# Projection, scalar and gate products of two token groups: plain fp32 in place of three split products

## The chip, the cores and the metric

The kernel runs on one core of one Trainium2 chip. The metric is the device time of one execution in microseconds (us), the median of several runs. The engines are named as in the profile: PE is TensorE (PEld its weight loads), DVE is VectorE, ACT is ScalarE, POOL is GpSimd, SP is SyncE, which here issues most DMAs. A measurement of this kernel can tell about 0.3% (13 us) from no change.

## The reference

One transformer layer on 1024 tokens plus 16 meta tokens, width 1024, in float32: a mixer with two branches of 8 heads (a gated delta rule, "gdn", and a forgetting attention, "fox"), then a feed-forward layer that looks up 16 experts for each of 8 heads and token ("peer"). Cut to what matters here:

```python
proj = h @ w_in                       # h = rms_norm(res); projections, 24 scalars, gates
qkv_a, z_a, b_a, a_a, qkv_b, f_b, gates = split_cols(proj, IN_SIZES)
...
o_a = rms_norm(gated_delta_rule(...), o_norm_a) * silu(z_a)
o_b = forgetting_attention(...)
y = einsum('blgc,gcd->blgd', o, w_branch)
res = res + sum(sigmoid(gates) * y, axis=2) @ w_out
# peer_ffn: route by top_k, then for the 128 (head, k) pairs of a token
act = gelu(einsum('thkd,td->thk', expert_u[idx], xb))
out = einsum('thk,thkd->td', gate_w * act, expert_v[idx])
```

## The kernel before

The eight blocks of 128 tokens are worked in three groups, blocks 0 to 1, 2 to 4 and 5 to 7 (`GROUPS`, line 26). In the code they are g = 0, 1, 2, in this text groups 1, 2 and 3. `mixer(g)` takes a group through these stages: the projections and the 8 heads (`scalars`, `proj_a`, `conv`, `proj_b`, `gdn`, `fox`, `gates`), the branches, the merge by `w_out`, and the ranking by `w_q`. While the merge and the ranking run, `prologue` normalises and transposes the next group's input into hT. For blocks 0 to 4 the experts are then gathered row by row: POOL issues a gather of 128 rows of `expert_u` or `expert_v`, DVE multiplies and sums the first kind (tiles G, h2p), and PE sums the second kind (`pv<-G,Zb`). This work is spread over all stages from the end of group 1 on. Blocks 5 to 7 go over all experts densely at the end (`dense`: `ua` over `u_t`, then `acc` over `expert_v`).

Products of width are made from two planes. A float32 value is split into a high part hi (rounded to fp32r, an fp32 form that PE takes in one pass) and a low part lo, and a product is hi·hi + hi·lo + lo·hi (`mm`, lines 411 to 420). The inputs' planes are in hT, which holds two planes of [128, 8, 384]. The weights are split as they come: `weights` (line 366) loads a piece wraw on SP's queue, ACT casts it to whi, and DVE or POOL, whichever the planner holds to be free sooner, subtracts to get wlo (line 393). A piece is one of eight k-slices of `w_a` (three 128-column parts of a head), `w_b` (four parts) or a gate slab `w_g`. The ring holds 7 raw pieces and 3 split ones, two pieces are split ahead of use (`D1`, line 62).

No order is written out by hand. `Weave` (line 223) is a planner that runs while the program is recorded: each stage is a generator, and the next step is that with the earliest ready time by the planner's own clocks and durations (`Engine`, `pe_time` and the like). Ties go by `prio`: gdn, then fox, then the projections, then the gates. So the projections fill what PE time the heads leave. Each engine then executes its instructions strictly in the recorded order and waits where an operand is not there.

Of the kernel before, what the change touches and what calls it, by code (L numbers as in the profile page):

```python
# [7 lines left out]
F32 = mybir.dt.float32  # L8
F32R = mybir.dt.float32r
# [4 lines left out]
OP = mybir.AluOpType  # L14
# [258 lines left out]
def _build(ctx, tc, nc, a, groups, dbg, peer):  # L273
# [86 lines left out]
    def bank(tag):  # L360
        return pl.ps.tile([P, 512], F32, name=tag, bufs=pl.banks[tag])
# [3 lines left out]

    def weights(srcs, by=None):


        size, RAW, RING, AHEAD = pl.depth
        todo = [(src, k, size // src.shape[-1]) for src in srcs for k in range(0, 8, size // src.shape[-1])]  # L370
        raws, have = [], []

        def room(t, i):
            src, k, n = todo[i]
            c = src.shape[-1]
            return t[:, :n * c].rearrange("p (k c) -> p k c", c=c)

        def load(n):
            while len(raws) < min(n, len(todo)):
                src, k, m = todo[len(raws)]  # L380
                raw = room(pl.wp.tile([P, size], F32, name="wraw", bufs=RAW), len(raws))
                sp.dma_start(raw, src[:, k:k + m, :])
                raws.append(raw)

        def fetch(n):
            while len(have) < min(n, len(todo)):
                i = len(have)
                load(i + RAW)
                raw = raws[i]
                hi = room(pl.wp.tile([P, size], F32R, name="whi", bufs=RING), i)  # L390
                lo = room(pl.wp.tile([P, size], F32R, name="wlo", bufs=RING), i)
                act.copy(hi, raw)
                (by or (pool if clk.t["pool"] + size * PCOST < clk.t["dve"] + size * 0.001 + PSL else dve)).tensor_tensor(lo, raw, hi, op=OP.subtract)
                raws[i] = None
                have.append((hi, lo))
        used = [0]

        def take():
            first = used[0]
            m = todo[first][2]  # L400
            used[0] += 8 // m

            def w(x, k, c0=0, c1=None):
                return have[first + k // m][x][:, k % m, c0:c1]
            w.need = lambda k: fetch(first + k // m + AHEAD)
            w.flat = lambda x: have[first][x].rearrange("p k c -> p (k c)")
            return w
        take.start = lambda: fetch(AHEAD)
        return take

    def mm(w, *sets):

        for k in range(8):
            w.need(k)
            for ps, lhs, rhs, then in sets:
                for n, (x, y) in enumerate(((0, 0), (0, 1), (1, 0))):
                    pe.matmul(ps, lhsT=lhs(x, k), rhs=rhs(y, k), start=(k == 0 and n == 0), stop=(k == 7 and n == 2))
                yield clk.when("pe", [w(x, k + 1) for x in range(2)], []) if k < 7 and lhs is sets[-1][1] else clk.t["pe"]
        for s in sets:
            s[3]()  # L420
# [43 lines left out]

    def rows_T(x, p, T8, c0, tag):

        for i in range(2):
            v = blocks(bank(tag))
            for k in range(4):
                tr(v[:, k, :p], x[:, (4 * i + k) * P:(4 * i + k + 1) * P], p)  # L470
            put(T8, slice(4 * i, 4 * i + 4), slice(c0, c0 + p), v[:, :, :p])
            yield
# [10 lines left out]
    def group(g):  # L483
        b0, b1 = groups[g]
        q = SimpleNamespace(g=g, b0=b0, nb=b1 - b0, mo=NM if g == 0 else 0, nkp=0 if g == 0 else NM + b0 * P)
        q.nw = q.nb * P
        q.T = q.mo + q.nw
        q.nbm = q.nb + (1 if q.mo else 0)
        q.last = b1 == NBLK
        q.two = 2 if g == 0 else 1  # L490
        q.bs = [(j, P, q.mo + j * P, b0 + j) for j in range(q.nb)]
        q.slots = ([(q.nb, NM, 0, -1)] if q.mo else []) + q.bs
        q.fl = PB[2] if g else 2
        return q

    def mixer(g):
        q = group(g)
        fl, b0, b1 = q.fl, q.b0, q.b0 + q.nb
        with ExitStack() as st:
# [7 lines left out]
                                + [a["w_o"][:, :, i * 512:(i + 1) * 512] for i in range(2)]  # L507
                                + [a["w_q"][:, :, i * 256:(i + 1) * 256] for i in range(8)])
            pl.banks = {"prj": PB[0], "bf": PB[1]} if g else {"prj": 3, "bf": 3}
# [3 lines left out]
            with sb("p0") as hp:  # L513
                q.oT = [hp.tile([P, 8, q.nw], F32, name=f"oT{br}") for br in range(0 if g else 2)]
                q.tok = lambda j: (lambda x, k: hT[:, x, k, q.mo + j * P:q.mo + (j + 1) * P])
                q.sg1 = hp.tile([P, 8, q.nw], F32, name="sg1") if g == 0 else None
                with sb("p1") as q.wk, banks("ps1") as pl.ps:
# [5 lines left out]
                    with sb("p1h") as q.wk:  # L523
# [17 lines left out]
                        for i in range(GF if g else 6):  # L541
                            wv.add(n("gates", i), gates(q, i // 3, i % 3), [n("gates", i - 1) if i else n("pb", H - 1)],
                                   prio=4)
                        wv.run(names + [n("gates", i) for i in range(GF if g else 6)])
                if g:
                    yp = st.enter_context(tpool(f"y_{g}", side="right", reuse_waits="tile"))
                    q.yF = yp.tile([P, 8, q.nw], F32, name="yF")
# [42 lines left out]
    def prologue(q, px, tags):  # L590
# [5 lines left out]
        for ss_ in batches:  # L596
# [10 lines left out]
            if q.mo:  # L607
                raw = px.tile([P, 8, 32], F32, name="wsr")
                act.dma_start(raw, a["w_s"])
            yield clk.when("act", xs[:1], [])  # L610
# [10 lines left out]
            if q.mo:  # L621
                act.copy(ws[0], raw)
                dve.tensor_tensor(ws[1], raw, ws[0], op=OP.subtract)
            yield
            for i, (j, C, c0, b) in enumerate(ss_):
                yield from rows_T(xs[i][:C], C, hT, c0, tags[at % len(tags)])
                at += 1

    def scalars(q):

        wk, g, n3 = q.wk, q.g, q.nbm
        if q.mo:
            act.activation(negA, negA, AF.Exp)
            dve.tensor_scalar(negA, negA, -1.0, None, op0=OP.mult)
            dve.tensor_scalar(qn, qn, P ** -0.5, None, op0=OP.mult)
        ps = bank("prj")
        for k in range(8):
            for n, (x, y) in enumerate(((0, 0), (0, 1), (1, 0))):
                pe.matmul(ps[:32, :q.T], lhsT=ws[x][:, k, :], rhs=hT[:, y, k, :q.T], start=(k == 0 and n == 0),
                          stop=(k == 7 and n == 2))  # L640
            yield clk.t["pe"]
# [72 lines left out]
    def proj_a(q, c, h):  # L714

        wk, T = q.wk, q.T
        wa = q.weights()
        raw = [wk.tile([P, T + 3], F32, name=f"raw{ty}", bufs=RW) for ty in range(3)]

        c.raw = raw  # L720

        def take(ps, ty):
            act.copy(raw[ty][:, 0:3], hal[:, ty, h, :])
            act.copy(raw[ty][:, 3:3 + T], ps[:, :T])
            act.copy(hal[:, ty, h, :], raw[ty][:, T:T + 3])
# [23 lines left out]
    def proj_b(q, c, h):  # L749
# [24 lines left out]
        for (j, C, c0, b) in q.slots:  # L774
            ps = bank("prj")
            if b < 0:
                sets.append((ps[:, 0:256], lambda x, k: hT[:, x, k, 0:P], lambda y, k: wb(y, k, 128, 384),
                             lambda ps=ps, j=j: meta(ps, j)))
            else:
                sets.append((ps, q.tok(j), lambda y, k: wb(y, k), lambda ps=ps, j=j, b=b: real(ps, j, b)))  # L780
# [279 lines left out]
    def gates(q, br, c):  # L1060
# [3 lines left out]
        def then(ps, i):  # L1064
# [80 lines left out]
    def rank(q):  # L1145
# [247 lines left out]
    def dense(b0, nb, held):  # L1393
# [5 lines left out]
        wscr = [dram.tile([P, P, P], F32, name=f"wscr{j}") for j in range(nb - 1)]  # L1399
        wt = ctx.enter_context(tpool("wt", side="right", reuse_waits="tile"))  # L1400
        W = []
        kept = wt.tile([P, NH, nw], F32, name="kept")
        with tpool("p4", reuse_waits="tile") as wk, \
# [4 lines left out]
            def inner():  # L1408
                for c in range(P):
# [8 lines left out]
                    ps = bank("ua")[:, :nw]  # L1418
                    yield from mm(w, (ps, lambda x, k: w(x, k), lambda y, k: hT[:, y, k, :nw], lambda: then(ps)))

# [176 lines left out]
```

## Time and profile before

| | us |
|---|---|
| time before, median of 3 runs | 4275.21 (4273.79 to 4283.71) |
| the profiled execution | 4281.61 |
| its span | 4279.9 |
| PE busy | 3785.7 (88%) |
| DVE busy | 2993.9 (70%) |
| POOL busy | 2265.0 (53%) |
| ACT busy | 1848.3 (43%) |

The share of busy time is a mean over stages that differ. Two stretches matter here. **Stretch A** is the projections, heads and gates of group 2, from its first scalar product (648.7 us) to the first branch product (1421.5 us). **Stretch B** is the same of group 3 (1719.9 to 2587.8 us). Together they are 1640.7 us, 38% of the span. A PE matmul's end is modelled in the profile, and matmuls overlap in the pipeline, so PE's busy time holds the tail of each; the time from one start to the next in a dense run is what a product occupies. A plain fp32 product stands in the trace as two matmul records, an fp32r one as one.

### The profile page before, as it was taken

To read this page: it belongs to the slowest core of one execution; us is meant where nothing else is said; L and a number is where in the kernel's file an instruction comes from. 1 tells how busy PE (TensorE), PEld (TensorE's weight loads), DVE (VectorE), ACT (ScalarE), POOL (GpSimd) and SP (SyncE) were. 2 spreads that over 40 slices of the span, in tenths; PEclk is the share of its full clock that TensorE was granted. 3 is DMA by queue.
4 is the path that set the end of the run, shared out by engine and by line. 5 is a ranking of instruction groups with operands and counts; after the bars stand their busy time and mean duration, and the time that the engine had idled before them with its cause. 6 is when DMAs were issued, how large, how long until landed. Compare 5 with 4: busy or idle time off the path is not lost. (4 is left out here: it accounts for less than half of the span.)

```text
span 4279.9 us, 65388 instructions
## 1 busy us (share of the span) xinstructions
PE 3785.7 (88%) x21126; PEld 2963.2 (69%) x21126; DVE 2993.9 (70%) x8230; ACT 1848.3 (43%) x4588; POOL 2265.0 (53%) x1935
## 2 busy tenths in 40 slices
PE   6999977888888978788898889779999998999998
PEld 5777866666656756556665567568888887776665
DVE  5565479989885667788788656579769565874443
ACT  4665443445443332344444433227666573332222
POOL 3222544665665656566575566564324354764553
PEclk9999988989999989899999999899999999999999
DMA  3232466677788988788788799888989999999997
GB/s 105 87 99 84 137 209 201 223 250 233 239 292 300 334 312 273 259 292 284 268 287 303 258 314 325 313 282 299 321 287 327 332 338 310 390 380 345 340 346 275
DMA packets 525066, 1161.20 MB, mean 271 GB/s; under 512 B 55281, under 2 KB 261137, under 8 KB 524337
## 3 DMA queue, kind: packets, MB, share of 16 engines
q0 software_dynamic: 186960, 679.04, 45.6%
q1 hardware_dynamic: 302464, 457.86, 31.8%
q10 hardware_dynamic: 35296, 20.12, 1.6%
q8 instruction: 166, 2.72, 0.3%
q14 instruction: 180, 1.47, 0.1%
HBM read 1081.73 MB, written 75.07 MB: 270 GB/s over the span
## 5 line engine op out<-in xcount | busy, mean ns | idle before, releaser
L185 POOL DMA_INDIRECT G<-in_expert_v_dram,idxT x640 | 729.9, 1141 | 729.0 <-PE pv L185 376.0
L185 POOL TENSOR_TENSOR wlo<-wraw,whi 128x384 fp32r<-128x384 f32 (+2 forms) x518 | 697.0, 1350 | 775.9 <-ACT whi L185 668.2
L185 POOL DMA_INDIRECT G<-in_expert_u_dram,idx x640 | 744.8, 1164 | 438.4 <-DVE G L185 144.1
L185 ACT CAST whi<-wraw 128x512 fp32r<-128x512 f32 (+2 forms) x1152 | 709.9, 629 | 596.6 <-PE prj L185 203.8
L185 DVE TENSOR_TENSOR wlo<-wraw,whi 128x512 fp32r<-128x512 f32 (+2 forms) x634 | 512.5, 815 | 609.1 <-ACT whi L185 522.1
L185 DVE SCALAR_TENSOR_TENSOR G<-G,h2p 128x1024 f32<-128x1024 f32 x618 | 800.6, 1299 | 64.6 <-DMA G<-in_expert_u_dram,idx 53.2
L185 PE MATMUL prj<-hT,whi 128*128 128x384 f32 (+2 forms) x2176 | 582.9, 354 | 43.6 <-ACT whi L185 33.2
L185 PE MATMUL ua<-hT,whi 128*128 128x384 f32 x2048 | 537.2, 343 | 16.9 <-ACT whi L185 16.9
L185 PE MATMUL pv<-G,Zb 128*32 128x512 f32 x2560 | 409.6, 622 | 54.2 <-DMA G<-in_expert_v_dram,idxT 52.6
L185 PEld LDWEIGHTS prj<-hT,whi 128*128 128x128 f32 x2176 | 384.4, 200 | 86.6 <-ACT whi L185 43.1
L185 PE MATMUL prj<-whi,hT 128*128 128x512 f32 (+1 forms) x1152 | 435.5, 417 | 3.8 <-ACT whi L185 2.7
L185 PEld LDWEIGHTS ua<-hT,whi 128*128 128x128 f32 x2048 | 364.8, 190 | 57.1 <-issue 35.2
L185 PE MATMUL prj<-hT,wlo 128*128 128x384 f32 (+2 forms) x1088 | 369.7, 340 | 24.4 <-POOL wlo L185 16.9
L185 PE MATMUL ua<-hT,wlo 128*128 128x384 f32 x1024 | 346.3, 338 | 4.0 <-DVE wlo L185 3.2
L185 PE MATMUL acc<-whi,Chi 128*128 128x512 f32 x768 | 311.2, 405 | 9.1 <-ACT whi L185 9.1
L185 PE MATMUL acc<-wlo,Chi 128*128 128x512 f32 x768 | 300.8, 392 | 1.8 <-POOL wlo L185 1.6
L185 PE MATMUL acc<-whi,Clo 128*128 128x512 f32 x768 | 300.4, 391 | 0.0
L185 PEld LDWEIGHTS prj<-whi,hT 128*128 128x128 f32 x1152 | 220.4, 194 | 52.9 <-issue 7.4
L185 PE MATMUL prj<-wlo,hT 128*128 128x512 f32 (+1 forms) x576 | 227.1, 394 | 24.2 <-POOL wlo L185 21.4
L185 PEld LDWEIGHTS prj<-hT,wlo 128*128 128x128 f32 x1088 | 215.2, 198 | 41.5 <-POOL wlo L185 31.0
L185 PEld LDWEIGHTS acc<-whi,Chi 128*128 128x128 f32 x768 | 144.7, 188 | 114.6 <-issue 75.5
L185 PEld LDWEIGHTS ua<-hT,wlo 128*128 128x128 f32 x1024 | 193.7, 189 | 8.2 <-DVE wlo L185 8.0
(316 smaller groups left out, 6912.9 us busy)
## 6 DMA issues: line engine op xcount, KB each, us to landing
wraw<-in_u_t_dram SPq DMA_DIRECT2D x256, 256.0 KB
wraw<-in_expert_v_dram SPq DMA_DIRECT2D x128, 512.0 KB
wraw<-in_w_b_dram SPq DMA_DIRECT2D x192, 256.0 KB
wraw<-in_w_a_dram SPq DMA_DIRECT2D x192, 192.0 KB
wraw<-in_w_q_dram SPq DMA_DIRECT2D x96, 256.0 KB
gscr<-Gl SPq DMA_DIRECT2D x122, 192.0 KB
Gr<-gscr SPq DMA_DIRECT2D x122, 192.0 KB
wraw<-in_w_g_dram SPq DMA_DIRECT2D x96, 192.0 KB
```

The lines of the kernel that those rows point to most:

```text
L185: return f(*a, **k)
```

## The change

In groups 2 and 3 the products with `w_a`, `w_b`, `w_g` and the 24 scalar columns are made of the whole float32 values: one plain fp32 product in place of three fp32r ones, and no whi and wlo for these weights. `weights` gets a count `whole`, the number of leading sources that are handed on as the raw piece. The inputs of groups 2 and 3 lie whole in a new buffer hW, half the size of hT; the planes of group 1 go to hT0, which lives only through group 1, and those for the ranking of group 3 and the dense phase to hD. Group 1, the branches, the merge, the ranking and the dense phase still use split products.

```diff
         size, RAW, RING, AHEAD = pl.depth
-        todo = [(src, k, size // src.shape[-1]) for src in srcs for k in range(0, 8, size // src.shape[-1])]
+        todo = [(src, k, size // src.shape[-1], i < whole) for i, src in enumerate(srcs)
+                for k in range(0, 8, size // src.shape[-1])]
...
                 i = len(have)
                 load(i + RAW)
                 raw = raws[i]
+                if todo[i][3]:
+                    have.append((raw,))
+                    continue
                 hi = room(pl.wp.tile([P, size], F32R, name="whi", bufs=RING), i)
                 lo = room(pl.wp.tile([P, size], F32R, name="wlo", bufs=RING), i)
                 act.copy(hi, raw)
@@ -397,11 +401,12 @@
...
         for k in range(8):
             w.need(k)
             for ps, lhs, rhs, then in sets:
-                for n, (x, y) in enumerate(((0, 0), (0, 1), (1, 0))):
-                    pe.matmul(ps, lhsT=lhs(x, k), rhs=rhs(y, k), start=(k == 0 and n == 0), stop=(k == 7 and n == 2))
-                yield clk.when("pe", [w(x, k + 1) for x in range(2)], []) if k < 7 and lhs is sets[-1][1] else clk.t["pe"]
+                pairs = ((0, 0),) if w.whole else ((0, 0), (0, 1), (1, 0))
+                for n, (x, y) in enumerate(pairs):
+                    pe.matmul(ps, lhsT=lhs(x, k), rhs=rhs(y, k), start=(k == 0 and n == 0),
+                              stop=(k == 7 and n == len(pairs) - 1))
+                yield clk.when("pe", [w(x, k + 1) for x in range(1 if w.whole else 2)], []) if k < 7 and lhs is sets[-1][1] else clk.t["pe"]
...
+            if plain:
+                copy(T8[:, 4 * i:4 * i + 4, c0:c0 + p], v[:, :, :p])
+            else:
+                put(T8, slice(4 * i, 4 * i + 4), slice(c0, c0 + p), v[:, :, :p])
...
+        q.hx = (lambda x, k, c0, c1: hW[:, k, c0:c1]) if g else (lambda x, k, c0, c1: hT0[0][:, x, k, c0:c1])
...
+                                whole=2 * H + len(gb[0]) if g else 0)
...
-                q.tok = lambda j: (lambda x, k: hT[:, x, k, q.mo + j * P:q.mo + (j + 1) * P])
+                if not g:
+                    hT0.append(planes(hp, "hT0", q.T))
+                    ws.extend(hp.tile([P, 8, 32], F32R, name=f"ws{i}") for i in range(2))
+                q.tok = lambda j: (lambda x, k: q.hx(x, k, q.mo + j * P, q.mo + (j + 1) * P))
...
+                if q.last and last < NBLK:
+                    hD.append(planes(held.enter_context(tpool("hD", side="right", reuse_waits="tile")), "hD", q.nw))
...
-                yield from rows_T(xs[i][:C], C, hT, c0, tags[at % len(tags)])
+                yield from rows_T(xs[i][:C], C, hW if q.g else hT0[0], c0, tags[at % len(tags)], q.g > 0)
...
+        pairs = ((0, 0),) if g else ((0, 0), (0, 1), (1, 0))
         for k in range(8):
-            for n, (x, y) in enumerate(((0, 0), (0, 1), (1, 0))):
-                pe.matmul(ps[:32, :q.T], lhsT=ws[x][:, k, :], rhs=hT[:, y, k, :q.T], start=(k == 0 and n == 0),
-                          stop=(k == 7 and n == 2))
+            for n, (x, y) in enumerate(pairs):
+                pe.matmul(ps[:32, :q.T], lhsT=wsF[:, k, :] if g else ws[x][:, k, :], rhs=q.hx(y, k, 0, q.T),
+                          start=(k == 0 and n == 0), stop=(k == 7 and n == len(pairs) - 1))
...
-            sets.append((ps[:, :T], lambda x, k, ty=ty: wa(x, k, ty * P, ty * P + P), lambda y, k: hT[:, y, k, :q.T],
+            sets.append((ps[:, :T], lambda x, k, ty=ty: wa(x, k, ty * P, ty * P + P), lambda y, k: q.hx(y, k, 0, q.T),
...
-        yield from wide(q, c1 - c0, lambda y, k: hT[:, y, k, q.mo:q.T], then)
+        yield from wide(q, c1 - c0, lambda y, k: q.hx(y, k, q.mo, q.T), then)
...
-        h2T = hT if b0 >= last else planes(wk, "h2T", q.nw)
+        h2T = hD[0] if b0 >= last else planes(wk, "h2T", q.nw)
...
-        wt = ctx.enter_context(tpool("wt", side="right", reuse_waits="tile"))
+        wt = ctx.enter_context(tpool("wt", reuse_waits="tile"))
...
-    hp = held.enter_context(tpool("hT", reuse_waits="tile"))
-    hT = planes(hp, "hT", max(group(g).T for g in range(len(groups))))
-    ws = [hp.tile([P, 8, 32], F32R, name=f"ws{i}") for i in range(2)]
+    inp = ExitStack()
+    hp = inp.enter_context(tpool("hT", reuse_waits="tile"))
+    hW = hp.tile([P, 8, max(group(g).nw for g in range(len(groups)))], F32, name="hW")
+    wsF = hp.tile([P, 8, 32], F32, name="wsF")
+    hT0, ws, hD = [], [], []
     for g in range(len(groups)):
         mixer(g)
+    inp.close()
```

The order of instructions follows from the planner. On PE, at the start of the second head of group 2, where `proj_a` of the next head (prj, 384 columns) stands among the transposes of gdn (bg) and of fox (bf), it was:

```order
L185 MATMUL bg_8425<-ident,cvv 128x128 x3
L185 MATMUL prj<-hT,whi 128x384 x2
L185 MATMUL prj<-hT,wlo 128x384
L185 MATMUL prj<-hT,whi 128x384 x2
L185 MATMUL prj<-hT,wlo 128x384
L185 MATMUL prj<-hT,whi 128x384 x2
L185 MATMUL prj<-hT,wlo 128x384
L185 MATMUL bg_8501<-ident,cv 128x128 x3
L185 MATMUL bf<-ident,qkr 128x128 x3
L185 MATMUL prj<-hT,whi 128x384 x2
```

and is now:

```order
L185 MATMUL bg_8827<-ident,cvv 128x128 x3
L185 MATMUL bf<-ident,qkr 128x128 x3
L185 MATMUL prj<-hW,wraw 128x384
L185 MATMUL bg_8850<-ident,cv 128x128 x3
L185 MATMUL prj<-hW,wraw 128x384 x3
L185 MATMUL bg_8890<-gam,Y 128x64 x3
L185 MATMUL bg_8896<-ident,cv 128x128 x3
L185 MATMUL prj<-hW,wraw 128x384 x3
L185 MATMUL bg_8923<-ident,X 128x128 x3
L185 MATMUL bf<-ident,qkr 128x128 x3
L185 MATMUL prj<-hW,wraw 128x384 x3
```

Each pair of rows hT,whi x2 and hT,wlo has become one product hW,wraw, and the steps of two gdn heads stand between them.

On POOL, early in stretch A, the subtractions stood between the gathers:

```order
L185 DMA G<-in_expert_u_dram,idx 128x1024 x4
L185 TENSOR_TENSOR wlo<-wraw,whi 128x384
L185 DMA G<-in_expert_u_dram,idx 128x1024
L185 TENSOR_TENSOR wlo<-wraw,whi 128x384
L185 DMA G<-in_expert_u_dram,idx 128x1024
L185 TENSOR_TENSOR wlo<-wraw,whi 128x384 x3
L185 DMA G<-in_expert_u_dram,idx 128x1024
L185 TENSOR_TENSOR wlo<-wraw,whi 128x384 x2
L185 TENSOR_TENSOR wlo<-wraw,whi 128x512
L185 DMA G<-in_expert_u_dram,idx 128x1024
```

and now there are gathers, with some products of an expert row by h2p (first steps of dot products that DVE made before):

```order
L185 DMA G<-in_expert_u_dram,idx 128x1024 x7
L185 TENSOR_TENSOR G<-G,h2p 128x1024
L185 DMA G<-in_expert_u_dram,idx 128x1024
L185 TENSOR_TENSOR G<-G,h2p 128x1024
L185 DMA G<-in_expert_u_dram,idx 128x1024 x10
L185 TENSOR_TENSOR G<-G,h2p 128x1024
L185 DMA G<-in_expert_u_dram,idx 128x1024 x3
L185 TENSOR_TENSOR G<-G,h2p 128x1024
L185 DMA G<-in_expert_u_dram,idx 128x1024 x18
L185 TENSOR_TENSOR G<-G,h2p 128x1024
```

Over the whole program POOL has 289 subtractions in place of 518 and 39 such products in place of 22, ACT 816 casts in place of 1152. The expert rows hardly move: PE has 16 more pv products in each of A and B, and 24 fewer in the dense phase on `expert_v`.

On SP, in the loads of the second and third weight of group 2, the DMA of a raw piece waited for the subtraction (on POOL or DVE) that last read its slot:

```order
L185 DMA wraw<-in_w_b_dram 128x512 [waits DMAHW1_49,Pool_49]
L185 DMA wraw<-in_w_b_dram 128x512 [waits DMAHW2_49,Pool_49]
L185 DMA decay_117<-GNT 8x384 [waits DMAHW3_49,Activation_49]
L185 DMA forget_120<-srow 8x656 [waits DMAHW4_49,DVE_49]
L185 DMA wraw<-in_w_b_dram 128x512 [waits DMAHW5_49,Pool_49]
L185 DMA wraw<-in_w_b_dram 128x512 [waits DMAHW6_49,Pool_49]
L185 DMA wraw<-in_w_a_dram 128x384 [waits DMAHW7_49,Pool_49]
```

and now it waits for PE, whose product is the last reader:

```order
L185 DMA wraw<-in_w_b_dram 128x512 [waits DMAHW1_49,PE_49]
L185 DMA wraw<-in_w_b_dram 128x512 [waits DMAHW2_49,PE_49]
L185 DMA decay_117<-GNT 8x384 [waits DMAHW3_49,Activation_49]
L185 DMA forget_120<-srow 8x656 [waits DMAHW4_49,DVE_49]
L185 DMA wraw<-in_w_b_dram 128x512 [waits DMAHW5_49,PE_49]
L185 DMA wraw<-in_w_b_dram 128x512 [waits DMAHW6_49,PE_49]
L185 DMA wraw<-in_w_a_dram 128x384 [waits DMAHW7_49,PE_49]
```

The loads stand in the same order and number (1232 rows in both programs); only what frees a slot has changed.

## Rows read from the trace of the kernel before

**Rows 1.** Busy time by engine in stretches A, B: start:end, length, busy us (instructions).
```profile
core 0: us, PE busy (x) PEld busy (x) DVE busy (x) ACT busy (x) POOL busy (x), PEclk, DMA share, GB/s
648.70:1421.50 772.80, 648.16 (x3456) 503.63 (x3454) 646.10 (x1837) 333.27 (x979) 467.14 (x391) 0.92 0.76 251
1719.90:2587.80 867.90, 744.36 (x4114) 523.24 (x4112) 664.56 (x2084) 354.96 (x1011) 544.68 (x465) 0.94 0.83 285
```

**Rows 2.** The same view of instructions touching whi alone: A, B, dense phase on `u_t`.
```profile
648.70:1421.50 772.80, 341.56 (x1025) 194.74 (x1025) 24.17 (x40) 91.66 (x169) 163.20 (x129) 0.92 0.76 251
...
1719.90:2587.80 867.90, 338.97 (x1025) 190.62 (x1025) 39.79 (x66) 92.11 (x169) 128.94 (x103) 0.94 0.83 285
...
2879.20:3614.20 735.00, 537.17 (x2048) 364.80 (x2048) 185.12 (x256) 156.13 (x256) 0.00 (x0) 0.99 0.92 315
```

**Rows 3.** Groups of PE instructions in A by shape: xcount | busy us, mean ns.
```profile
L185 PE MATMUL prj<-hT,whi 128*128 128x384 f32 x640 | 187.5, 375 | 12.8 <-ACT whi L185 11.1 <-ACT junk L185 1.2 <-issue 0.3
L185 PE MATMUL prj<-whi,hT 128*128 128x512 f32 x384 | 154.0, 440 | 0.7 <-ACT whi L185 0.7
```

**Rows 4.** Timeline of PE, split products back to back: start us, us taken.
```profile
2965.23 0.51 PE L185 MATMUL ua<-hT,whi 128*128 128x384 f32 x2
...
2965.75 0.51 PE L185 MATMUL ua<-hT,whi 128*128 128x384 f32 x2
...
3734.52 0.39 PE L185 MATMUL acc<-whi,Chi 128*128 128x512 f32 x1
...
3735.20 0.39 PE L185 MATMUL acc<-whi,Chi 128*128 128x512 f32 x1
```

**Rows 5.** Timeline of PE, one plain fp32 product of 512 columns and its successor.
```profile
1127.91 1.02 PE L185 MATMUL bf<-kall,qT 128*128 128x512 f32 x2
1128.77 0.78 PE L185 MATMUL bg<-X,AA 128*128 128x64 f32 x6
```

**Rows 6.** Waits in A: who for whom, us in total, times, longest us.
```profile
POOL wlo L185 <- ACT whi L185: 167.5, 67, 6.3
...
PEld prj L185 <- POOL wlo L185: 29.1, 34, 2.9
...
DVE wlo L185 <- ACT whi L185: 26.7, 13, 11.2
...
PE prj L185 <- POOL wlo L185: 16.5, 22, 2.5
...
PEld prj L185 <- ACT whi L185: 15.2, 6, 5.9
PE prj L185 <- ACT whi L185: 11.8, 4, 5.0
```

**Rows 7.** Waits in B, the same view.
```profile
DVE wlo L185 <- ACT whi L185: 68.4, 37, 11.4
...
PEld pv L185 <- DMA G<-in_expert_v_dram,idxT: 51.1, 30, 8.6
...
PEld prj L185 <- ACT whi L185: 25.2, 11, 9.2
PEld prj L185 <- POOL wlo L185: 23.7, 28, 2.1
...
PE prj L185 <- ACT whi L185: 20.1, 8, 8.8
PE prj L185 <- POOL wlo L185: 14.5, 23, 1.8
```

**Rows 8.** The expert dot products, a group of DVE, in A.
```profile
L185 DVE SCALAR_TENSOR_TENSOR G<-G,h2p 128x1024 f32<-128x1024 f32 x192 | 255.1, 1330 | 13.3 <-DMA G<-in_expert_u_dram,idx 9.7 <-issue 3.6
```

**Rows 9.** The same group in the dense phase on `u_t`.
```profile
L185 DVE SCALAR_TENSOR_TENSOR G<-G,h2p 128x1024 f32<-128x1024 f32 x98 | 119.2, 1218 | 2.7 <-DMA G<-in_expert_u_dram,idx 1.7 <-issue 1.0
```

**Rows 10.** The expert outputs, a group of PE over the whole span.
```profile
L185 PE MATMUL pv<-G,Zb 128*32 128x512 f32 x2560 | 409.6, 622 | 54.2 <-DMA G<-in_expert_v_dram,idxT 52.6
```

More of the change, by code (lines that the diff above doesn't have):

```diff
@@ L364, in blocks, with weights @@
         return ps.rearrange("p (j c) -> p j c", c=P)
-    def weights(srcs, by=None):
+    def weights(srcs, whole=0, by=None):
         size, RAW, RING, AHEAD = pl.depth
-        todo = [(src, k, size // src.shape[-1]) for src in srcs for k in range(0, 8, size // src.shape[-1])]
+        todo = [(src, k, size // src.shape[-1], i < whole) for i, src in enumerate(srcs)
+                for k in range(0, 8, size // src.shape[-1])]
         raws, have = [], []
         def room(t, i):
-            src, k, n = todo[i]
+            src, k, n, _ = todo[i]
             c = src.shape[-1]
@@ L379, in load @@
             while len(raws) < min(n, len(todo)):
-                src, k, m = todo[len(raws)]
+                src, k, m, _ = todo[len(raws)]
                 raw = room(pl.wp.tile([P, size], F32, name="wraw", bufs=RAW), len(raws))
@@ L399, in take @@
             first = used[0]
-            m = todo[first][2]
+            m, whole_ = todo[first][2:]
             used[0] += 8 // m
@@ L404, in w @@
                 return have[first + k // m][x][:, k % m, c0:c1]
+            w.whole = whole_
             w.need = lambda k: fetch(first + k // m + AHEAD)
@@ L463, in rsqrt, with rows_T @@
         return y
-    def rows_T(x, p, T8, c0, tag):
+    def rows_T(x, p, T8, c0, tag, plain=False):
         for i in range(2):
@@ L470, in rows_T @@
                 tr(v[:, k, :p], x[:, (4 * i + k) * P:(4 * i + k + 1) * P], p)
-            put(T8, slice(4 * i, 4 * i + 4), slice(c0, c0 + p), v[:, :, :p])
+            if plain:
+                copy(T8[:, 4 * i:4 * i + 4, c0:c0 + p], v[:, :, :p])
+            else:
+                put(T8, slice(4 * i, 4 * i + 4), slice(c0, c0 + p), v[:, :, :p])
             yield
@@ L507, in mixer @@
                                 + [a["w_o"][:, :, i * 512:(i + 1) * 512] for i in range(2)]
-                                + [a["w_q"][:, :, i * 256:(i + 1) * 256] for i in range(8)])
+                                + [a["w_q"][:, :, i * 256:(i + 1) * 256] for i in range(8)],
+                                whole=2 * H + len(gb[0]) if g else 0)
             pl.banks = {"prj": PB[0], "bf": PB[1]} if g else {"prj": 3, "bf": 3}
@@ L607, in prologue @@
             if q.mo:
-                raw = px.tile([P, 8, 32], F32, name="wsr")
-                act.dma_start(raw, a["w_s"])
+                act.dma_start(wsF, a["w_s"])
             yield clk.when("act", xs[:1], [])
@@ L621, in prologue @@
             if q.mo:
-                act.copy(ws[0], raw)
-                dve.tensor_tensor(ws[1], raw, ws[0], op=OP.subtract)
+                act.copy(ws[0], wsF)
+                dve.tensor_tensor(ws[1], wsF, ws[0], op=OP.subtract)
             yield
             for i, (j, C, c0, b) in enumerate(ss_):
-                yield from rows_T(xs[i][:C], C, hT, c0, tags[at % len(tags)])
+                yield from rows_T(xs[i][:C], C, hW if q.g else hT0[0], c0, tags[at % len(tags)], q.g > 0)
                 at += 1
@@ L776, in proj_b @@
             if b < 0:
-                sets.append((ps[:, 0:256], lambda x, k: hT[:, x, k, 0:P], lambda y, k: wb(y, k, 128, 384),
+                sets.append((ps[:, 0:256], lambda x, k: q.hx(x, k, 0, P), lambda y, k: wb(y, k, 128, 384),
                              lambda ps=ps, j=j: meta(ps, j)))
@@ L1418, in inner @@
                     ps = bank("ua")[:, :nw]
-                    yield from mm(w, (ps, lambda x, k: w(x, k), lambda y, k: hT[:, y, k, :nw], lambda: then(ps)))
+                    yield from mm(w, (ps, lambda x, k: w(x, k), lambda y, k: hD[0][:, y, k, :nw], lambda: then(ps)))
             def gates_of(b, dst):
```

## The prediction

> **What bounds the kernel now.** I read the busy times by stretch first, because the change touches only the projections of groups 2 and 3. In stretch A of 772.8 us PE is busy 648.2, DVE 646.1, POOL 467.1; in B of 867.9 us it is 744.4, 664.6 and 544.7 [rows 1]. No engine fills its stretch. Four engines run a fixed order and wait for each other: PE stands idle 772.8 - 648.2 = 124.6 us in A and 123.5 in B, 248 together, and more than that is lost inside busy spans, since a busy matmul's span holds its pipeline tail. Second, the part that goes: the chain raw piece, ACT cast, subtraction, product [rows 2]. Third, the waits [rows 6, 7]: POOL and DVE stand in front of a subtraction until ACT has cast (167.5 and 26.7 us in A), and PE stands until whi or wlo is there.
>
> **Products.** A group has 320 products of 384 columns and 192 of 512 that change: the whi rows hold two of a product's three parts, 640 / 2 and 384 / 2 [rows 3]. Three split parts of 384 columns start 2965.75 - 2965.23 = 0.52 us after the last three, of 512 columns 3735.20 - 3734.52 = 0.68 us [rows 4]. One plain fp32 product of 512 columns holds PE for 1128.77 - 1127.91 = 0.86 us [rows 5]; for 384 columns I take 0.86 x 384 / 512 = 0.645, the cost being by column. So each product costs more: 0.125 us on 328 (the 8 scalar products count as 384 wide) and 0.18 us on 192, 41.0 + 34.6 = 75.6 us a group, 151 us in both. The granted clock was 0.92 in A and 0.94 in B [rows 1], so 151 / 0.93 = **+162 us** of PE time. Bounds: 151 (all at 2.4 GHz) and 162.
>
> Rows 5 shows 0.86 us for a product of 512 columns, 3.8 times the 0.227 us of one split part. The Trainium skill (FP8 and Floating Point Precision, TensorE Precision Notes) gives true fp32 four passes of the array; with four times the split part the extra PE time would be 213 us instead of 162, an estimate from that page, and the sum below would end near the old time. The row decides.
>
> **PE's waits for whi and wlo.** They go with the operands. On the matmul itself they are 16.5 + 11.8 us in A and 20.1 + 14.5 in B, 63 us; on the weight load ahead of it 29.1 + 15.2 and 25.2 + 23.7, 93 us [rows 6, 7]. A load that waits holds its matmul, whose predecessor's modelled tail covers part of the wait in the matmul's row. So I take **-93 us**, with 63 as the other end. What is late next is the raw piece. Seven slots stay; a slot is now free when PE has read it, and SP stands at that DMA until then, with the head's loads (gam, kall, vall, ncr) and the routing's behind it. The lead is six pieces; 168 pieces in 772.8 us are 4.6 us each, 28 us of lead on average and 6 x 1.9 = 12 us where products of 384 columns run back to back. I cost it at nothing under that cover; if it were gone, each head would wait about once, at the 8.8 us of the longest wait for whi [rows 7] 16 x 8.8 = 141 us.
>
> **Helpers that come late.** In A and B the change takes from ACT 91.7 + 92.1 us of casts, from POOL 163.2 + 128.9 us of subtractions and from DVE 24.2 + 39.8 us [rows 2]. DVE also loses its stands in front of them, 26.7 + 68.4 us [rows 6, 7]. And its dot products are slower while POOL subtracts: 1330 ns in A against 1218 ns in the dense phase, where POOL makes none [rows 2, 8, 9]; 192 x 0.112 = 21.5 us in A, and by the count of subtractions (103 against 129) some 17 in B. So DVE is relieved by about 64 + 95 + 38 = 197 us of 1640.7, and POOL, no longer standing in front of casts, can issue gathers earlier, for which PE's pv loads wait 51.1 us in B [rows 7]. What reaches PE of this is unknown: no row shows the stretch without its subtractions. Of PE's 248 us idle, 155 are left after the 93, nearly all waits for DVE, ACT and gathers. Bounds: 0 (the lateness is the latency of each step, not a queue) and -155. I take half, **-78 us**: DVE works 84% of A, which is a queue, but gdn and fox are chains whose steps have latency whatever the load.
>
> The dots are slowed only where POOL reads too, as rows 8 and 9 show. The Trainium skill (SBUF — State Buffer, Who interferes with whom) says that a DVE instruction with two SBUF inputs and a GpSimd one that reads SBUF exclude each other for a whole instruction. Were every subtraction such a block, DVE would get up to 292 us back from it, an estimate by that page, where the dots show 38; that would favour the strong gain below.
>
> **The clock.** The granted clock is 0.92 to 0.94 in A and B and 0.99 in the dense phase, where PE has fewer gaps [rows 1, 2]. With fewer gaps in A and B it should rise: 0.015 on 1393 busy us is **-20 us**. Bounds: 0, and -70 if it reached 0.98.
>
> **Dense phase.** 24 pv products leave the phase on `expert_v` and 4 enter the one on `u_t`: 20 products, 40 records of 409.6 / 2560 = 0.16 us [rows 10], **-6 us**. What they cost in A and B (32 products, 64 x 0.16 = 10 us) lies in gaps of PE and is in the half taken above. The copies in place of splits for hW lie in the ranking, beside its products; nothing. The moved pools change which tiles share an address; the first loads of `u_t` stand behind the same stores on SP, nothing.
>
> **The sum.** 162 - 93 - 78 - 20 - 6 = -35 us against the profiled run's 4281.6: 4246.6. The median is 6.4 us lower than that run: **4240 us**.
>
> **Rivals.** (1) *PE becomes the bound (slower).* The products grow by 162 us, PE loses only the waits for whi and wlo, and the helpers are as late as before, since each gdn and fox step now also stands behind longer products (0.86 us for 0.68). Then 162 - 78 (the mean of 63 and 93) - 6 = +78: 4353 us. It decides when helpers and clock give back less than 162 - 93 - 6 = 63 us of the 98 taken. For it speaks that PE is already busy 84% and 86%; against it that DVE is as busy in A and gets lighter. (2) *No change:* about those 63 us come back, 4275 us. (3) *Strong gain:* DVE's queue was the cause of the idle time, and all 155 us go: 162 - 93 - 155 - 20 - 6 = -112, 4163 us. For it speaks that DVE loses 197 us; against it that PE's products now fill what it frees. (4) *Late weights:* raw slots held by PE; 4240 + 141 = 4381 us. Against it: the 12 to 28 us of lead. That the change does not do what it says is out: the order on PE shows one product for three.
>
> **How the numbers follow.** Forecast (4205 to 4262) 0.40, strong gain 0.22, no change 0.14, PE bound 0.21, late weights 0.03. A difference under 0.3% (13 us) can't be told from none. Faster by more than that: 0.40 + 0.22 = 0.62; within: 0.14; slower: 0.24. The range takes in the strong gain and most of the PE-bound case: 4150 to 4345.
>
> **What would show it.** In the profile of the changed kernel: a plain prj product of 512 columns starts 0.86 us before its successor; no waits for whi or wlo in A and B; DVE's dots there near 1220 ns; granted clock above 0.94; the idle time of PE before bg, bf and pv smaller. I am wrong if stretch A or B is longer at the same idle time of PE before bg and bf (then rival 1), or if PE waits there for landings of wraw (rival 4).

## The result

The changed kernel takes 4226.4 us (median of 4 runs, 4215.5 to 4229.8) against 4274.5 of the kernel before: ratio 0.9877, interval 0.9852 to 0.9901. The forecast was 4240, faster; the gain is 48 us where 35 were forecast. Its profiled execution took 4228.9 us, span 4227.2.

Stretches A and B after, same view as [rows 1]:

```profile
core 0: us, PE busy (x) PEld busy (x) DVE busy (x) ACT busy (x) POOL busy (x), PEclk, DMA share, GB/s
643.30:1398.00 754.70, 682.62 (x2965) 397.37 (x2964) 546.03 (x1787) 273.40 (x840) 340.48 (x289) 0.95 0.80 267
1688.40:2542.20 853.80, 786.99 (x3624) 430.45 (x3623) 583.05 (x2047) 284.94 (x838) 428.10 (x382) 0.97 0.87 299
```

A is 18 us shorter, B 14. PE is busy 34 and 43 us longer in them and idle 72.1 and 66.8 us, where it was 124.6 and 123.5 [rows 1]. DVE lost 100 and 82 us of busy time, POOL 127 and 117. Of the span's 52.7 us, 32 came from A and B, 5 from before A, 8 and 10 from the branches, merges and rankings behind A and B; the dense phase grew by 3 (16 more on `u_t`, 13 less on `expert_v`).

The price of a plain product of 384 columns, read as in [rows 5]: two records, and the next product starts 0.65 us after the first. The row ahead of it, a transpose of fox, is for a reading further down.

```profile
1198.99 0.27 PE L185 MATMUL bf<-ident,srow 128*16 128x128 f32 x1
1199.10 0.81 PE L185 MATMUL prj<-hW,wraw 128*128 128x384 f32 x2
1199.75 0.52 PE L185 MATMUL bg<-X,AA 128*128 128x64 f32 x3
```

PE's waits before projections, A and then B. The whi and wlo rows of [rows 6, 7] are gone; what is left as a wait for something is ACT, whose reading of the last result (junk) frees PE's buffer, and a few late pieces (wraw):

```profile
PEld prj L185 <- issue: 51.1, 194, 1.5
...
PEld prj L185 <- ACT junk L185: 12.3, 13, 2.2
...
PE prj L185 <- ACT junk L185: 5.7, 7, 1.9
...
PEld prj L185 <- DMA wraw<-in_w_a_dram: 3.1, 1, 3.1
...
PEld prj L185 <- issue: 59.5, 220, 1.3
...
PEld prj L185 <- ACT junk L185: 10.5, 11, 1.9
...
PEld prj L185 <- DMA wraw<-in_w_a_dram: 10.0, 2, 9.7
...
PE prj L185 <- ACT junk L185: 4.9, 10, 1.7
```

The largest rows, "issue", are idle time of the weight load alone, about 0.27 us each time, in which it waits for nothing that the profile shows. The matmul has no such row in A or B, so they are not read as standing time of PE.

DVE's dot products and two of its convolution steps in A, as in [rows 8]. The dots fell from 1330 to 1217 ns; the convolution steps cv and cvv of before stand below those of the changed kernel:

```profile
L185 DVE SCALAR_TENSOR_TENSOR G<-G,h2p 128x1024 f32<-128x1024 f32 x186 | 226.0, 1217 | 13.5 <-DMA G<-in_expert_u_dram,idx 7.6 <-issue 3.9 <-PE bf L185 1.9
L185 DVE SCALAR_TENSOR_TENSOR cv<-raw,cw,cv 128x384 f32<-128x384 f32 x48 | 27.5, 613 | 0.0
L185 DVE SCALAR_TENSOR_TENSOR cvv<-raw,cw,cvv 128x384 f32<-128x384 f32 x24 | 14.6, 608 | 0.0
...
L185 DVE SCALAR_TENSOR_TENSOR cv<-raw,cw,cv 128x384 f32<-128x384 f32 x48 | 38.0, 830 | 0.0
L185 DVE SCALAR_TENSOR_TENSOR cvv<-raw,cw,cvv 128x384 f32<-128x384 f32 x24 | 26.8, 1116 | 0.0
```

The dots in B, before and after. What stands behind the second bar is DVE's idle time in front of them, most of it for gathered rows:

```profile
L185 DVE SCALAR_TENSOR_TENSOR G<-G,h2p 128x1024 f32<-128x1024 f32 x177 | 233.2, 1320 | 25.5 <-DMA G<-in_expert_u_dram,idx 21.0 <-issue 3.3 <-PE sk L185 1.2
...
L185 DVE SCALAR_TENSOR_TENSOR G<-G,h2p 128x1024 f32<-128x1024 f32 x178 | 216.5, 1219 | 20.9 <-DMA G<-in_expert_u_dram,idx 19.2 <-DMA G<-in_expert_v_dram,idxT 1.4
```

One place in A of the changed kernel costs what no row of before shows. POOL makes six products of expert rows by h2p in one go; DVE, PE and ACT at the same time (start us, us, idle before and its releaser):

```profile
994.47 13.84 POOL L185 TENSOR_TENSOR G<-G,h2p 128x1024 f32<-128x1024 f32 x6
...
997.01 11.34 DVE L185 TENSOR_SCALAR vi<-ix 128x32 f32<-128x32 uint32 x1
...
1010.61 0.69 PE L185 MATMUL bf<-ident,qkr 128*128 128x128 f32 x2 [8.76 <-ACT qkr L185]
...
1010.16 0.69 ACT L185 ACTIVATE qkr<-qkr,f_r 128x128 f32<-128x128 f32 x2 [14.56 <-DVE f_r L185]
```

A DVE step on 32 elements stands for 11.3 us until POOL's last product is done; the f_r behind it on DVE holds ACT for 14.6 us, and ACT holds PE for 8.8.

To follow the time I use two sums over the trace. The first goes by starts: the time from each matmul's start to the next is split into the product's own price, what the lower clock (1.2 of 2.4 GHz) adds to it, and the rest, a wait, put to the tile that was waited before. (A gap under 25 ns counts as price.) The second takes every DVE instruction that overlapped one of POOL's two-input instructions, and sums what it took beyond the median of its own kind, if over 0.15 us; I call it DVE's **stretch**. For A and B together, in us:

| | before | price only (e1) | changed | no POOL products (e5) |
|---|---|---|---|---|
| products at full clock | 1096.8 | 1265.9 | 1272.2 | 1277.1 |
| lower clock | 72.7 | 62.8 | 48.2 | 31.9 |
| waits before prj | 156.7 | 58.3 | 58.0 | 58.3 |
| waits before bg and bf | 260.7 | 229.1 | 188.9 | 158.1 |
| waits before pv | 50.8 | 58.9 | 38.2 | 38.4 |
| sum of these rows | 1637.7 | 1675.0 | 1605.5 | 1563.8 |
| DVE's stretch | 165.1 | 134.0 | 33.0 | 0.0 |
| median of the runs | 4274.5 | 4320.1 | 4226.4 | 4169.6 |

One part of the first sum is not what its name says. In the kernel before, a split product that comes right behind a product of the heads starts, mostly, 0.02 to 0.03 us after that product's last record, where a plain product starts 0.11 us after it (the transpose above); and the product after it starts 0.08 us late: the three parts below take 0.61 us where [rows 4] has 0.52.

```profile
1298.19 0.27 PE L185 MATMUL bf<-ident,srow 128*16 128x128 f32 x1
1298.21 0.60 PE L185 MATMUL prj<-hT,whi 128*128 128x384 f32 x2
1298.65 0.34 PE L185 MATMUL prj<-hT,wlo 128*128 128x384 f32 x1
1298.82 0.33 PE L185 MATMUL prj<-hT,whi 128*128 128x384 f32 x1
```

The late start occurs 355 times in A and B of before and is nearly always of the same size, 0.08 to 0.09 us, so I read it as a matter of where records begin and not as a wait for another engine. By the rule of the sum it stands all the same among the waits before prj, with 31.6 us, and some 22 us of it are missing from the products of before. Behind plain products it does not occur.

### The profile page after: what moved, and what is told of

It reads as the page before. It is cut to its first block, busy times and chain, and to the rows that moved or that the text cites. A ratio compares the mean times of both kernels' runs of the same rounds, so it can differ in the third digit from the quotient of the medians.

```text
span 4227.2 us, 62093 instructions
## 1 busy us (share of the span) xinstructions
PE 3847.9 (91%) x20086; PEld 2756.5 (65%) x20086; DVE 2803.3 (66%) x8105; ACT 1716.7 (41%) x4270; POOL 1982.1 (47%) x1723
## 4 chain that ended last, share of the span: by engine, by line
PE 38%; DMA 9%; DVE 8%; issue 5%; POOL 3%; ACT 2%; ACTq 0%; SPq 0%; POOLq 0%; DVEq 0%
PE acc L185 11%; PE prj L185 9%; PE ua L185 7%; PE pv L185 5%; DMA G<-in_expert_v_dram,idxT 3%; PE bg L185 2%; POOL G L185 2%; PE bf L185 2%; DVE G L185 2%; PE w L185 1%; DMA wraw<-in_u_t_dram 1%; POOL wlo L185 1%; DMA s<-sscr 1%; DVE wlo L185 1%; DVE e L185 1%
## 5 line engine op out<-in xcount | busy, mean ns | idle before, releaser
L185 ACT CAST whi<-wraw 128x512 fp32r<-128x512 f32 (+2 forms) x816 | 526.6, 659 | 551.6 <-PE prj L185 189.2
L185 POOL TENSOR_TENSOR wlo<-wraw,whi 128x512 fp32r<-128x512 f32 (+2 forms) x289 | 401.7, 1397 | 463.1 <-ACT whi L185 382.9
L185 PE MATMUL ua<-hD,whi 128*128 128x384 f32 x2048 | 538.5, 344 | 16.7 <-ACT whi L185 16.5
L185 PE MATMUL prj<-hW,wraw 128*128 128x384 f32 x1280 | 486.4, 515 | 29.4 <-DMA wraw<-in_w_a_dram 11.5
L185 PEld LDWEIGHTS ua<-hD,whi 128*128 128x128 f32 x2048 | 365.0, 190 | 58.7 <-issue 36.0
L185 PE MATMUL prj<-wraw,hW 128*128 128x512 f32 x768 | 377.6, 606 | 0.8 <-ACT raw L185 0.8
L185 PE MATMUL ua<-hD,wlo 128*128 128x384 f32 x1024 | 347.3, 339 | 7.9 <-DVE wlo L185 7.4
L185 PEld LDWEIGHTS prj<-hW,wraw 128*128 128x128 f32 x1280 | 240.3, 201 | 174.7 <-issue 23.7
L185 PEld LDWEIGHTS ua<-hD,wlo 128*128 128x128 f32 x1024 | 193.8, 189 | 11.9 <-DVE wlo L185 11.9
L185 PE MATMUL prj<-oTs,whi 128*128 128x384 f32 (+1 forms) x768 | 183.7, 326 | 9.5 <-DVE oTs L185 6.3
```

What stands on the lines that cost most here:

```text
L185: return f(*a, **k)
```

## The experiments

**Theory 1** is that of the prediction: the plain products cost PE more than they free it of waits, and only the lighter helpers make a gain of it. Its rivals: the relief is worth nothing, or it is ACT's, or POOL's, or that of DVE's own work.

**e1_price_only: the new products, all the old helper work.** Every whole piece is still cast and subtracted; nobody reads the result.

```diff
-                if todo[i][3]:
-                    have.append((raw,))
-                    continue
...
-                have.append((hi, lo))
+                have.append((raw,) if todo[i][3] else (hi, lo))
```

> The changed kernel, but every weight piece of groups 2 and 3 is still cast by ACT and subtracted by POOL or DVE (1152 casts and 518 + 634 subtractions, the counts of the kernel before); nobody reads these planes, the products take the raw piece. It has the price of the plain products and PE's freedom from whi and wlo, and none of the relief of the helpers. Theory 1 (the prediction's: PE pays 162 us, gets 63 to 93 back from waits for whi and wlo, and only the lighter helpers turn this into a gain): 4275 + 162 - 78 - 6 = about 4350, between 4335 and 4370, DVE's dot products in stretches A and B near 1330 ns. Rival A (the relief is worth nothing, the gain is the freed order of PE alone): within 15 us of the changed kernel's 4226. Rival B (half of each): near 4285.

Measured: 4320.1 us, ratio 1.0106 (1.0083 to 1.0129). Slower than before, so the first half of theory 1 holds: alone, the new products lose 46 us. It is 30 less than expected: waits before bf fell from 95.2 to 61.4 us although the helpers were as loaded as before, and the clock gave back 10. The relief, from here to the changed kernel, is worth 94 us, net of what the 19 more products of expert rows on POOL in the changed kernel cost (39, here 20). DVE's dots in A stay long:

```profile
L185 DVE SCALAR_TENSOR_TENSOR G<-G,h2p 128x1024 f32<-128x1024 f32 x180 | 234.7, 1304 | 15.3 <-DMA G<-in_expert_u_dram,idx 10.1 <-DMA G<-in_expert_v_dram,idxT 3.2 <-PE prj L185 1.4
```

**e1_casts_only: of the helper work ACT's casts alone.**

```diff
+                hi = room(pl.wp.tile([P, size], F32R, name="whi", bufs=RING), i)
+                act.copy(hi, raw)
+                raws[i] = None
                 if todo[i][3]:
                     have.append((raw,))
                     continue
...
```

> The changed kernel with ACT's casts of groups 2 and 3 kept (1152) but no subtractions there (POOL 288, DVE 528); nobody reads the cast plane. Theory 1 in its form that DVE and POOL are the helpers that count: within 15 us of 4226, dots near 1220 ns. Rival (ACT's queue was what came late): more than half of the distance between the changed kernel and the one with all helper work, 4280 or more.

Measured: 4257.2 us (4239.8 to 4266.2), ratio 0.9951 (0.9935 to 0.9967). Between the two: the 336 casts cost about 31 us, the subtractions the other 63, if the two add up. The form of theory 1 in which only DVE and POOL count allowed 15 us; ACT's share is a third.

**e1_pool_subs and e1_dve_subs: all helper work, the subtractions of groups 2 and 3 on one engine.** On top of the edit of e1_price_only:

```diff
-                (by or (pool if ...
+                (pool if todo[i][3] else by or (pool if ...
```

(and `dve if todo[i][3]` in the other).

> As the kernel with all helper work kept, but every subtraction of the pieces of groups 2 and 3 stands on POOL (POOL 628, DVE 524); DVE makes none of them and stands in front of none. Theory 1a (DVE's own work and stands are what counts): near the changed kernel, 4226 to 4260. Theory 1b (what counts is that DVE is slowed while POOL subtracts, and that POOL stands in front of casts with gathers behind it): as slow as with all helper work or slower, 4340 to 4390, dots at 1330 to 1400 ns.

> The changed kernel with all casts and subtractions of the pieces of groups 2 and 3 still made (nobody reads the planes), every subtraction there on DVE and none on POOL (POOL 298, DVE 854 over the program). With the mix of both engines it was 4320.1 us, with all on POOL 4340.2, with casts alone 4257.2. If a subtraction hurts mainly through POOL (DVE's two-input instructions slowed beside it, gathers behind it): dots at 1220 ns and 4270 to 4300, although DVE has some 330 subtractions of 0.56 to 0.69 us, 200 us, more work in stretches A and B. If DVE's own queue is what counts: 4340 to 4380, slower than with all on POOL. Both equal: near 4320.

Measured: 4340.2 us (ratio 1.0154, 1.0132 to 1.0177) and 4316.6 (1.0081, 1.0056 to 1.0107). With POOL doing all of them DVE has 110 subtractions fewer than in e1_price_only, and the kernel is 20 us slower; DVE's stretch rises to 197.6 us (read from the slowest of the five executions, 4361.0 us). So a subtraction on POOL is not free for DVE. The second result, no change, seemed to say that both places cost the same. It doesn't: the planner, seeing DVE full, gave POOL 67 products of expert rows, and DVE's stretch was still 106.9 us. Hence e10, below.

**e3_ring9: nine raw slots for seven.**

```diff
-D1 = (512, 7, 3, 2)
+D1 = (512, 9, 3, 2)
```

> The changed kernel with 9 raw slots in place of 7 in groups 2 and 3. The trace of the changed kernel has 4.6 us (A) and 12.0 us (B) of PE waiting for a piece whose load stood on SP's queue until PE had freed the slot. If the late weights of rival 4 are a small rest, these go and the time falls by 5 to 15 us, to 4211 to 4221; if they hide in other waits (the heads' loads behind SP's standing DMA), by 20 to 50; if the lead of seven slots is enough, within 5 us of 4226.

Measured: 4232.7 us, ratio 0.9913 (0.9888 to 0.9938). No gain: two more slots did not help. The one long wait for a piece of w_a in B (9.7 us) is still there, at 7.8.

**e6_group1: group 1 in plain fp32 too.** hT0 whole, `whole` for every group.

```diff
-                                whole=2 * H + len(gb[0]) if g else 0)
+                                whole=2 * H + len(gb[0]))
...
-                    hT0.append(planes(hp, "hT0", q.T))
+                    hT0.append(hp.tile([P, 8, q.T], F32, name="hT0"))
```

> The changed kernel with group 1 in plain fp32 too (256 + 16 tokens; no experts run beside it, DVE has no dot products there). Price on PE in group 1, from the same rates by column: 192 x 0.085 + 128 x 0.075 + 128 x 0.18 + 64 x 0.075 = 54 us; PE's waits for whi and wlo there are only a few us. Theory 1 (the relief is worth something where the helpers' queues are shared with the expert work, so less here): slower by 10 to 40 us, 4236 to 4266. Rival (lighter helpers are worth as much per subtraction here, 94 us for 336 pieces, 47 us for 168): within 10 us of 4226, or faster.

Measured: 4259.6 us, ratio 0.9961 (0.9948 to 0.9975): 33 us slower than the changed kernel, as theory 1 has it. Products in group 1 took 60 us more and the lower clock 10, waits 29 less. POOL's 133 us of subtractions went, and with them 40.6 us of DVE's stretch; it bought less than the products cost. That this is so because no expert work competes for DVE there is argued, not shown.

**e7_rate400: expert work earlier.** `RATE = 400e3` for `360e3`.

> The changed kernel with the planner's constant for the gather rate raised from 360e3 to 400e3, so that it records expert work earlier: 560 pv products in stretches A and B in place of 500, 492 in the dense phase in place of 576. In the dense phase PE is full and 84 pv products with two records of 0.16 us are 27 us. If PE's idle time in A and B (285 us by the spacing of starts) can take them: faster by 10 to 27 us, 4200 to 4216. If the gathers are late for them (PE's pv loads wait): within 10 us or slower.

Measured: 4291.4 us, ratio 1.0034 (1.0020 to 1.0048), 65 us slower than the changed kernel; both expectations too good. The dense phase gained 31 us, A and B lost 62. In B the waits for gathered rows doubled (changed kernel: 37.3 and 19.9 us):

```profile
PEld pv L185 <- DMA G<-in_expert_v_dram,idxT: 84.6, 54, 6.0
PE pv L185 <- DMA G<-in_expert_v_dram,idxT: 45.4, 32, 5.1
```

Recorded this early, the expert outputs do not fill PE's idle time in A and B; their rows come late.

**e5_no_pool_products: POOL's 39 products of expert rows back on DVE.**

```diff
-DSL = -2
+DSL = -100
```

> The changed kernel with POOL's 39 products of an expert row by h2p given back to DVE (0 on POOL); so POOL makes no two-input instruction in A and B at all. DVE gets 39 x 1.22 = 48 us more over the whole program and ACT 39 sums less; some 18 dots that ran at 2.2 us beside POOL's instructions return to 1.22, 18 us. If what is left of the slowdown beside POOL still reaches PE: faster by 5 to 15 us than 4226. If DVE's queue is what counts: slower by 5 to 20. Otherwise within 5.

Measured: 4169.6 us, ratio 0.9738 (0.9705 to 0.9771): 57 us faster than the changed kernel, nearly four times the most that was expected. A is 707.0 us, and the clock granted there rises to 0.98:

```profile
654.40:1361.40 707.00, 665.43 (x2965) 388.80 (x2964) 536.05 (x1813) 260.44 (x816) 313.92 (x276) 0.98 0.84 286
1638.10:2498.00 859.90, 785.55 (x3631) 429.73 (x3630) 582.01 (x2059) 285.23 (x844) 413.92 (x383) 0.97 0.86 300
```

DVE is busy less than in the changed kernel (546.0 in A) though it makes 14 dots more there. By the profiled executions A gave 48 us, the dense phase on `u_t` 17 and the stages between A and B 14; B took 6, and what lies before A 11. Of these only A's share is larger than what a mere reordering moved in one stage (e11 below).

**e9_before_no_products: is that a cost of the change?** The same edit on the kernel before.

> The kernel before with its 22 products of an expert row by h2p taken from POOL and given to DVE (0 on POOL); its subtractions stay (POOL 518, DVE 634). In the trace of before POOL's products stand in the dense phase (16 of them), one in A, none in B; in the changed kernel 13 stand in A and 6 in B, and without them it is 57 us faster. If those 57 us are a cost that the change itself brought in (more POOL products, because the planner takes POOL for free): this kernel within 20 us of the kernel before's 4275. If POOL's products cost the same whatever stands beside them, 57 us for 39: 22 x 1.46 = 32 us faster, 4243.

Measured: 4264.7 us, ratio 0.9977 (0.9964 to 0.9990): only 10 us. So most of the 57 us came in with the change: 4274.5 to 4226.4 with POOL's products, a gain of 48; 4264.7 to 4169.6 without them, a gain of 95. In A, before had one such product and the changed kernel has 13. The 17 us on `u_t` are not explained by this: before has 16 of the products there, the changed kernel 17, and this run gained nothing there (739.3 us for 735.0).

**e10_dve_subs_no_products: DVE overfull, POOL without two-input instructions in A and B.** e1_dve_subs with `DSL = -100`.

> As the kernel with every cast and subtraction of groups 2 and 3 kept and all subtractions there on DVE (4316.6 us), and POOL's 67 products given to DVE as well, so that POOL runs no two-input instruction in stretches A and B, while DVE has some 200 us more subtractions there than in the changed kernel. If DVE's stretching beside POOL's two-input instructions is what the relief consisted of: 4316.6 minus some 60 to 100, 4220 to 4260, although DVE is fuller than in any other run. If DVE's own queue is what counts: 4316 or more.

Measured: 4259.7 us, ratio 0.9967 (0.9953 to 0.9981), 57 us faster than e1_dve_subs, at the upper end of what the stretch predicts, with 169 subtractions on DVE in A alone. The work itself counts as well: with the casts on ACT and the subtractions on DVE it is 90 us slower than e5. A and B are even shorter than e5's together, 1511.5 to 1566.9 us, and the time comes back later, since the planner put 132 of the pv products off into the dense phase, which takes 1528.1 us where e5 takes 1388:

```profile
650.30:1363.00 712.70, 655.75 (x2838) 400.90 (x2837) 574.29 (x1882) 337.29 (x989) 226.92 (x200) 0.95 0.71 229
1638.60:2437.40 798.80, 751.27 (x3493) 430.18 (x3492) 632.48 (x2155) 356.56 (x1002) 358.82 (x314) 0.97 0.82 279
2723.90:4252.00 1528.10, 1435.86 (x7570) 1088.09 (x7570) 989.80 (x2331) 633.30 (x1231) 772.47 (x643) 0.97 0.96 343
```

**e8_no_pool_two_input: e5, and nearly all subtractions of all stages on DVE** (`PSL = -100`).

> The changed kernel without POOL's products and with nearly all subtractions of all stages on DVE (POOL 5, DVE 811), so that POOL does little but issue gathers after the start. In group 1 DVE is stretched by 40.6 us beside POOL's 133 us of subtractions, in the dense phase on expert_v by 68.4 beside 96. If DVE has room there: faster than the 4169.6 of the version without products by 10 to 40 us. If the subtractions on DVE (284 more, about 0.6 to 1.3 us each, 200 us) come late for PE in group 1 and on expert_v: slower than it by 10 to 50.

Measured: 4194.4 us, ratio 0.9813 (0.9788 to 0.9837), 25 us slower than e5. DVE's stretch is gone everywhere, but the stages behind B (branches, merge and ranking of group 3) are 15 us longer in sum, and A and B are 17 and 15 longer than e5's with the same work of the projections in them. Each of these is within what a reordering moves (e11), and why they are all longer stays open.

**e11_other_order: e5 in another order.** The planner's allowance behind ACT is 0.16 us for 0.15.

> The changed kernel without POOL's products (4169.6 us), its work left as it is, but recorded in another order: one of the planner's constants, the time it allows from ACT's end to a waiter's start, is 0.16 us in place of 0.15. All instructions of the projections are the same; A has 4 pv products more, the dense phase 8 fewer. How much does the order alone move? If the gain without POOL's products is a matter of what stretches DVE: within 15 us of 4169.6. If the order that the planner happens to write is worth as much as the effects read here: off by 25 us or more, and then single differences under that are not to be read.

Measured: 4172.1 us, ratio 0.9745 (0.9714 to 0.9777), 2.5 us from e5. A reordering of equal work moved the whole by little, and e5's time is no accident of one order. Single stages moved more: branches, merge and ranking of group 3 went from 279.0 to 298.1 us and A from 707.0 to 713.6. So a difference of up to 19 us in one stage can be a matter of order.

## Why the prediction came out right, step by step

**What bounds the kernel: right.** Four engines wait for each other; PE's idle time fell from 248 to 139 us, and no engine fills its stretch after the change either.

**Products: right.** 0.65 us for 384 columns as worked out. By their own price the projections of A and B rose by 152 us (151 forecast at 2.4 GHz). The rest of the 175 in the table is 16 more pv products in each stretch (7 us) and, for the most part, the 22 us that the table puts elsewhere in before. The 213 us that the prediction estimated from the Trainium skill (FP8 and Floating Point Precision, TensorE Precision Notes) are not borne out by these rows.

**Waits for whi and wlo: right, the size between its two ends.** Waits before prj fell by 98.7 us in the table, but 31.6 us of that are the late starts shown above. That leaves 67, nearer to the 63 of the prediction's other end than to its 93. The fall is as large in e1_price_only, where the helpers were as busy as before: this part belongs to the product's form. Rival 4, late weights, is out: the loads of w_a's pieces hold PE's weight load for 3.1 and 10.0 us, where the rival had 141, and nine slots recovered nothing. (The longest wait for whi in [rows 7] is 9.2 us, on the weight load, not the 8.8 that the rival took; it would have made 147.)

**Helpers: the size right, for two wrong reasons.** Waits before bg, bf and pv fell by 84.4 us, forecast 78. The 78 were half of an interval, chosen and not worked out. The step that failed is the sizing of what DVE gets back: the prediction counted only the dots, 38 us. Many kinds of DVE instructions were stretched beside POOL's subtractions (the dots are 40 us of 165), and the stretch fell by 132 us. And a term was missing: the order on POOL, shown ahead of the prediction, had products of expert rows where the subtractions had been, 39 for 22, and the prediction gave them no price. Taking them away is worth 57 us; 19 of the 39 stand in A and B. The two errors have opposite signs and nearly cancel, and that the sum came out so close is luck. Without the second, the result is 4169.6, next to the strong gain of rival 3 (4163), but that too is a likeness of numbers: the rival has PE's idle time in A and B gone, and e5 still has 116 us of it. Its reason, DVE's queue, holds in part: e10 gives DVE 67 products more than e1_dve_subs and is 57 us faster, so what POOL does beside DVE counts for more there than the length of DVE's queue.

The other way in which a lighter POOL could help, earlier gathers, is small here: waits before pv, which are waits for gathered rows, fell by 12.6 of the 84.4 us, and DVE waits in front of its dots as long as before in A (13.3 and 13.5 us) and 5 us less in B. No run separates the two.

What makes 13 products of 30 us in sum cost 48 us in A is only partly shown: by starts, 35 us are waits and 13 clock; the stop at 994 us is 9 of them; DVE's stretch in A was 22 us, and ACT, which has to sum each such row, had 13 sums of 1.07 us more. How the rest builds up was not settled.

**Rival 1, PE the bound.** It is the case that e1_price_only built, 4320 us instead of 4353. Its condition, that helpers and clock give back less than 63 us, was not met: 94.

**Clock: right.** 0.92 and 0.94 became 0.95 and 0.97; by starts 24.5 us, forecast 20.

**Dense phase and the rest: missed by 14 us in sum.** Forecast -6 for the dense phase, measured +3; and 23 us came from before A and from the stages between, where nothing was forecast. The phase on `expert_v` fell by 13 us, but the one on `u_t` grew by 16, and without POOL's products (e5) it is back at 733.8 us. Single stages move by up to 19 us between orders of equal work; what else is in it was not followed.

## What to carry to other kernels

Exact products in two records can beat three split ones although they cost PE more, where the casts and subtractions that they save stand in queues with other urgent work; in group 1, with no expert work beside it, they cost 33 us in sum. When work is taken off an engine, look in the new order for what a planner puts in its place, and price that as if it were part of the change. And a two-input instruction on POOL is to be charged to DVE as well: in A and B of the kernel before, DVE was stretched by 165 us beside 295 us of them.

## What was not expected of the hardware

A small DVE instruction can stand through several POOL instructions in a row, not only through the one that runs: vi<-ix began 0.2 us into the second of six products of 2.3 us each and ended with the sixth, 11.3 us. In e3_ring9 another step, two inputs of 6 elements a partition, took 12.05 us; it began half a microsecond ahead of a run of five and ended with it:

```profile
1001.66 11.52 POOL L185 TENSOR_TENSOR G<-G,h2p 128x1024 f32<-128x1024 f32 x5
...
1001.17 12.05 DVE L185 TENSOR_TENSOR g_rt<-g_rt,sse 128x6 f32<-128x6 f32 x1
```

The Trainium skill (SBUF — State Buffer, Who interferes with whom) says that, where the two engines contend for their shared ports, whichever issues first holds them for its whole instruction and the other is blocked fully. These rows agree that DVE is held, for 11.3 and 12.05 us, and not slowed in proportion, and show besides that a run of POOL instructions was not broken up for it. By that rule the step in e3_ring9, which began first, would not have been held; why it was, no row shows.
